# Gate blocks and recurrence values moved to the front of a hybrid decoder layer, as wide blocks with partly seven products

## The chip, the cores and the metric

The kernel runs on one core of one Trainium2 chip. The metric is the device time of one execution in microseconds. TensorE multiplies, VectorE and ScalarE do the elementwise work, POOL (GpSimd) does some of it, SyncE's queue issues the loads of weights. All data is float32; a float32 operand is split into a rounded high part and a remainder ("low"), and a product is made of three passes: high by high, high by low, low by high.

## The reference, cut to what matters

One decoder layer on 256 positions of width 2048:

```
a    = RMSNorm(x)
proj = a @ w_in                        # 17408 columns: q, k, v of attention (3 x 3072),
                                       # q, f, i, g of the recurrence (4 x 1024),
                                       # gate_a, gate_r (2 x 2048)
attn = dilated window attention of 3 head groups, 8 heads, mixed by their denominators
r    = gated linear recurrence over chunks, 8 heads, RMSNorm per head, times silu(g)
y    = sigmoid(gate_a) * (attn @ w_attn_branch) + sigmoid(gate_r) * (r @ w_hgrn_branch)
h    = x + RMSNorm(y @ w_mix_out)
ff   = (silu(gt) * up) @ w_ffn_down,  gt, up = split(RMSNorm(h) @ w_ffn_gate_up)
out  = h + RMSNorm(ff)
```

Every gate is one linear projection of `a`, so gates can be computed at any time before `y`.

## The kernel before

Weights stream once from DRAM. The unit of streaming is 512 KB (a chunk); two chunks share one raw buffer and there are three such buffers. ScalarE rounds a chunk (L242), VectorE takes the remainder (L243), TensorE multiplies. A narrow block ("N", `Block`) is 512 output columns: eight steps of 12 products, two halves of 128 positions, each accumulating in its own PSUM bank. A "W" block is 256 columns computed transposed, four steps. A wide block (`Wide`) is 1024 columns as two groups of 512, one step for each pair of 128-row weight tiles; its raw step is 1 MB. In a plain wide step there are 24 products (2 halves x 2 groups x 2 tiles x 3 passes). In a seven-product step the 2 x 2 block product is done with seven block products instead of eight, 21 in all: VectorE forms sums of the weights (L310, L316, L317), ScalarE rounds them (L315, L318, and L320 for the plain weights still needed), VectorE takes the remainders (L321 `wl`, L322 `dl`), and sums of the activations (`seven_sums`, L374 to L385) stand ready. `gather` collects four of the banks at the last such step, and the block's evacuation adds the rest.

Work is issued in one fixed order. The main loop runs over all steps; at step n it issues the split of step n+2, the load of what is three raw buffers ahead, the products of step n, and then advances generators by one turn each: `evacs` (evacuations of finished blocks), `turns` (transposes of y), and two `lanes` (opening, recurrence and attention on `lanes[0]`, attention and gate sigmoids on `lanes[1]`). Each engine executes its instructions in that order, so the step in which a generator's turn is issued sets where it stands in an engine's queue. A tile's buffer is given to the next tile when all accesses of the old one are done. `flush` issues all remaining turns of a queue at once.

The order of blocks is: output gate g (two N blocks, beside them `opening` with the norms and small tables, L515), f and q of the recurrence (W), its values i (two N blocks, COL_IR), then twice v (three N), q and k (W), then gate_a and gate_r (eight N blocks), then for each of four column blocks j the attention branch and the recurrence branch (8 row tiles, four steps each), the mix projection (`mix`, four N blocks), the first gate and up block (N), ten wide blocks of the feed-forward part, two wide blocks of 22 steps of the down projection. The recurrence starts when the second q block is evacuated; attention for half of the heads starts when that half's last k block is evacuated, two heads in each lane, each head 16 turns. Gates that are evacuated before the heads are done are held as they are (`waiting`) and get their sigmoid behind the heads on `lanes[1]` (`gate_sigmoids`, L934), since Exp and Sigmoid need different ScalarE tables. `evac_g` (L626) multiplies with `gainr`, loaded by `opening` at L518. The mix projection takes y through `yT[0].after(turns)`, which pulls a missing piece (`turned`, L422; `put`, L407) at once.

In the down projection every step first splits its activations: `prep_act` (L1176) puts high and low parts, and for a seven-product step forms the sums, all ahead of the weights' split. At the end `finish` sums, squares, normalises and stores the last columns.

Of the kernel before, what the change touches and what calls it, by code (L numbers as in the profile page):

```python
# [19 lines left out]
P = 128  # L20
# [16 lines left out]
H7 = (0, 1, 2)  # L37
GATE_UP = [(3, 0), (4, 0), (0, 1), (5, 0), (1, 1), (6, 0), (2, 1), (7, 0)]
DOWN = [[(m, m in by7) for m in range(KF // 2)] for by7 in (range(4, 20, 3), range(3, 19, 3))]

N_RAW, N_SPLIT, AHEAD, WARM, BRIDGE = 6, 3, 2, 8, 6
# [20 lines left out]
class Wide:  # L62
# [7 lines left out]
    def __init__(self, w, cols, order, xs, seven, evac, prep=None, pre=None, turn=1):  # L70
# [3 lines left out]
        self.bank, self.open, self.rest = {}, set(), None  # L74
# [3 lines left out]
def tile_hybrid_block(ctx: ExitStack, tc: tile.TileContext, t, out):  # L78
# [8 lines left out]
    auxp = ctx.enter_context(tc.tile_pool(name="auxp", bufs=4, space=PSUM))  # L87
    ctx.enter_context(tc.manual_schedule())
# [19 lines left out]
    def p3(s, dtype, n, bufs, tag=None):  # L108
        return act_pool[0].tile([P, n], dtype, tag=tag or s, bufs=bufs, name=nm(s))
# [48 lines left out]
    ph1 = ExitStack()  # L158
    kp = ph1.enter_context(tc.tile_pool(name="kp", bufs=1, reuse_waits="tile"))
    fp = ph1.enter_context(tc.tile_pool(name="fp", bufs=1, reuse_waits="tile"))  # L160

    act_pool = []

    def fslot(s):
        return fp.tile([P, 1024], F32, tag="f", bufs=15, name=nm(s))

    def ptile(s):
        pool, n = (act_pool[0], 2) if act_pool else (fp, 5)
        return pool.tile([P, 512], F32, tag="p", bufs=n, name=nm(s))
# [13 lines left out]
    blocks, chunks, pairs = [], [], []  # L183
    wides, steps = [], []

    def add(*args, **kw):
        b = Block(*args, **kw)
        blocks.append(b)
        for c in range(b.steps):
            chunks.append([b, c, None, None, None])  # L190
# [15 lines left out]
    def parts(j):  # L206

        return (slice(0, 512), slice(512, 1024)) if j == 0 else (slice(0, 1024),)

    def load(j):  # L210
        if j >= len(chunks):
            load_wide(j - len(chunks))
            return
        b, c = chunks[j][:2]
        if j % 2 == 0:
            pairs.append(stream.tile([P, 2048], F32, tag="raw", bufs=N_RAW // 2, name=nm("raw")))
        raw = pairs[j // 2][:, j % 2 * 1024 : j % 2 * 1024 + 1024]
        rows = b.per * P
        src = b.w[c * rows : (c + 1) * rows, b.col : b.col + b.width]
        src = src.rearrange("(k p) c -> p k c", p=P)  # L220
        dst = raw.rearrange("p (k c) -> p k c", k=b.per)
        n = len(parts(j))
        for i in range(n):
            ks = slice(i * b.per // n, (i + 1) * b.per // n)
            nc.sync.dma_start(dst[:, ks, :], src[:, ks, :])
        chunks[j][2] = raw
# [4 lines left out]
    def split(j, only=None):  # L231
        if j >= len(chunks):
            split_wide(j - len(chunks))
            return
        raw = chunks[j][2]
        if chunks[j][3] is None:
            w = wslot()
            chunks[j][3:] = [w[:, :1024], w[:, 1024:]]
        wh, wl = chunks[j][3:]
        for n, k in enumerate(parts(j)):  # L240
# [4 lines left out]
    def multiply(j, sides=(0, 1)):  # L245
        b, c = chunks[j][:2]
        wh, wl = (w.rearrange("p (k c) -> p k c", k=b.per) for w in chunks[j][3:])
        if b.banks is None:
            b.banks = [acc_bank() for _ in range(2)]
        for s in sides:  # L250
# [23 lines left out]
    def add_wide_block(*args, **kw):  # L274
        b = Wide(*args, **kw)
        wides.append(b)
        for i in range(len(b.order)):
            steps.append([b, i, None, None])

    def load_wide(n):  # L280
        if n % 2 or n // 2 >= len(steps):
            return
        n //= 2
        b, i = steps[n][:2]
        m = b.order[i][0]
        raw = stream.tile([P, 2048], F32, tag="raw", bufs=N_RAW // 2, name=nm("raw"))
        for g, col in enumerate(b.cols):
            src = b.w[2 * m * P : (2 * m + 2) * P, col : col + 512]
            nc.sync.dma_start(
                raw[:, g * 1024 : (g + 1) * 1024].rearrange("p (k c) -> p k c", k=2),  # L290
                src.rearrange("(k p) c -> p k c", p=P),
            )
        steps[n][2] = raw

    def split_wide(n):

        if n >= len(steps):
            return
        b, i, raw = steps[n][:3]
        m, by7 = b.order[i]  # L300
        if b.prep:
            b.prep(m, by7)
        hi, lo = wslot(), p3("wl", F32R, 2048, 3)
        if not by7:
            nc.scalar.activation(hi, raw, AF.Copy)  # L305
            nc.vector.tensor_sub(lo, raw, hi.bitcast(F32))  # L306
            steps[n][3] = hi, lo
# [10 lines left out]
        nc.scalar.activation(hi[:, 1024:], s[:, 1024:], AF.Copy)  # L318
        dhi, dlo = p3("dh", F32R, 1536, 1), p3("dl", F32R, 1536, 1)
        nc.scalar.activation(dhi, d, AF.Copy)  # L320
        nc.vector.tensor_sub(lo, s, hi.bitcast(F32))  # L321
        nc.vector.tensor_sub(dlo, d, dhi.bitcast(F32))  # L322
        steps[n][3] = hi, lo, dhi, dlo

    def multiply_wide(n, sides=(0, 1), groups=(0, 1)):
        b, i = steps[n][:2]
        m, by7 = b.order[i]
        parity = wides.index(b) % 2
# [1097 lines left out]
```

## Time and profile before

| | us |
|---|---|
| median of three runs | 1753.55 (1753.36 to 1753.64) |
| the profiled execution | 1753.68 |
| its span, first to last instruction | 1751.9 |
| TensorE busy | 1730.3 (99%) |
| VectorE busy | 1265.1 (72%) |
| ScalarE busy | 885.0 (51%) |
| POOL busy | 74.1 (4%) |

Matmul ends are modelled and matmuls are pipelined, so TensorE's busy share hides short waits; the time between the starts of products tells more. Instruction rows give start, duration, engine, line, out<-in, shape, and in square brackets the idle time before it with what ended it. Window rows give the length, then the busy time and the number of instructions of PE (TensorE), PEld (its weight loads), DVE (VectorE), ACT (ScalarE) and POOL, then the granted clock, and the DMA share and rate.

### The profile page before, as it was taken

The page shows a single profiled execution, that of the slowest core. Times are in us where ns is not written, and L with a number is a line of the kernel's source. Part 1 is how long each engine was busy: PE and PEld are TensorE (multiplying, and loading weights), DVE is VectorE, ACT ScalarE, POOL GpSimd, SP SyncE. Part 2 cuts the span into 40 slices and gives each one's busy share as a digit, 9 for nine tenths or more (in the row PEclk, how much of TensorE's full clock was granted, in tenths as well). Part 3 has the DMA queues.
Part 4 walks back from the last instruction along what each step waited for, and adds up shares of the span by engine and source line. Part 5 has one row for each costly group of instructions (what it writes and reads, how often), then busy time and mean ns, then how long its engine had stood idle before and what let it go on. Part 6 is the DMA issues. An engine that isn't in the chain of part 4 may idle for free.

```text
span 1751.9 us, 21592 instructions
## 1 busy us (share of the span) xinstructions
PE 1730.3 (99%) x8424; PEld 1449.0 (83%) x8424; DVE 1265.1 (72%) x1372; ACT 885.0 (51%) x1050; POOL 74.1 (4%) x54
## 2 busy tenths in 40 slices
PE   9999999999999999999999999999999999999997
PEld 7888888888888888888888877888888888878775
DVE  5657657877546775544565577888888888888887
ACT  6545445344444444454444465555555555565563
POOL 0002404300000000000000000000000000000000
PEclk9999999999999999999999999999999999999999
DMA  7655444455455554455555745555555555656553
GB/s 265 204 191 193 144 162 151 145 165 182 159 169 169 189 188 161 159 175 193 194 183 189 268 157 203 194 192 193 204 206 204 201 194 192 223 181 218 183 183 117
DMA packets 201223, 325.92 MB, mean 186 GB/s; under 512 B 10096, under 2 KB 76832, under 8 KB 201120
## 3 DMA queue, kind: packets, MB, share of 16 engines
q1 hardware_dynamic: 198848, 319.41, 54.2%
q10 hardware_dynamic: 2272, 5.12, 0.8%
q8 instruction: 66, 1.08, 0.2%
q14 instruction: 37, 0.30, 0.1%
HBM read 322.40 MB, written 2.10 MB: 185 GB/s over the span
## 4 chain that ended last, share of the span: by engine, by line
PE 82%; DVE 12%; ACT 3%; issue 2%; DMA 1%; POOL 0%; SPq 0%; DVEq 0%; ACTq 0%
PE acc L115 65%; PE aux L115 16%; DVE wl L306 3%; DVE wl L321 1%; DVE dl L322 1%; DVE a L411 1%; DVE sum L310 1%; ACT w L318 1%; DVE w L243 1%; DVE sum L317 0%; DVE sum L316 0%; ACT w L242 0%; DVE w L667 0%; ACT so L384 0%; DVE s L379 0%
## 5 line engine op out<-in xcount | busy, mean ns | idle before, releaser
L243 DVE TENSOR_TENSOR w<-raw,w 128x1024 fp32r<-128x1024 f32 (+1 forms) x353 | 444.2, 1260 | 366.4 <-ACT w L242 364.3
L242 ACT ACTIVATE w<-raw 128x1024 fp32r<-128x1024 f32 (+1 forms) x353 | 373.0, 1057 | 483.1 <-PE acc L115 472.1
L115 PE MATMUL acc<-w,xT 128*128 128x512 f32 x1728 | 407.9, 394 | 0.0
L115 PEld LDWEIGHTS acc<-w,xT 128*128 128x128 f32 x1728 | 325.1, 190 | 65.7 <-DVE w L243 0.3
L115 PE MATMUL acc<-xT,w 128*128 128x512 f32 (+1 forms) x2048 | 365.5, 340 | 0.0
L115 PEld LDWEIGHTS acc<-xT,w 128*128 128x128 f32 x2048 | 314.8, 189 | 46.1
L306 DVE TENSOR_TENSOR wl<-raw,w 128x2048 fp32r<-128x2048 f32 x82 | 187.4, 2285 | 19.9 <-ACT w L305 19.9
L305 ACT ACTIVATE w<-raw 128x2048 fp32r<-128x2048 f32 x82 | 156.4, 1908 | 59.0 <-PE aux L115 27.0
L115 PE MATMUL acc<-w,hT 128*128 128x512 f32 x622 | 182.5, 392 | 1.5 <-DVE w L243 1.2
L115 PEld LDWEIGHTS acc<-w,hT 128*128 128x128 f32 x622 | 115.8, 188 | 27.0 <-DVE w L243 2.5
L115 PE MATMUL aux<-w,hT 128*128 128x512 f32 x430 | 135.6, 389 | 0.0
L321 DVE TENSOR_TENSOR wl<-sum,w 128x2048 fp32r<-128x2048 f32 x42 | 96.3, 2292 | 47.3 <-ACT w L318 47.3
L115 PEld LDWEIGHTS aux<-w,hT 128*128 128x128 f32 x430 | 80.7, 188 | 16.8
L315 ACT ACTIVATE w<-sum 128x1024 fp32r<-128x1024 f32 x42 | 44.6, 1063 | 96.3 <-DVE sum L310 92.0
L115 PE MATMUL acc<-w,yT 128*128 128x512 f32 x384 | 88.0, 390 | 0.2 <-DVE w L243 0.2
L115 PEld LDWEIGHTS acc<-w,yT 128*128 128x128 f32 x384 | 71.9, 188 | 15.4 <-DVE w L243 0.6
L115 PE MATMUL acc<-w,a 128*128 128x512 f32 x268 | 83.7, 389 | 0.0
L115 PE MATMUL aux<-w,a 128*128 128x512 f32 x268 | 83.7, 389 | 0.0
L115 PE MATMUL aux<-wl,hT 128*128 128x512 f32 x215 | 83.6, 389 | 0.0
L115 PE MATMUL acc<-wl,hT 128*128 128x512 f32 x215 | 83.6, 389 | 0.0
L322 DVE TENSOR_TENSOR dl<-raw,dh 128x1536 fp32r<-128x1536 f32 x42 | 73.5, 1751 | 0.0
L320 ACT ACTIVATE dh<-raw 128x1536 fp32r<-128x1536 f32 x42 | 61.9, 1473 | 0.0
(263 smaller groups left out, 2016.9 us busy)
## 6 DMA issues: line engine op xcount, KB each, us to landing
raw<-in_w_in SPq DMA_DIRECT2D x271, 512.0 KB, 4.5
raw<-in_w_ffn_gate_up SPq DMA_DIRECT2D x176, 512.0 KB, 4.4
raw<-in_w_ffn_down SPq DMA_DIRECT2D x88, 512.0 KB, 4.9
raw<-in_w_mix_out SPq DMA_DIRECT2D x32, 512.0 KB, 4.9
raw<-in_w_attn_branch SPq DMA_DIRECT2D x16, 512.0 KB, 4.6
raw<-in_w_hgrn_branch SPq DMA_DIRECT2D x16, 512.0 KB, 4.6
hx<-in_x ACTq DMA_DIRECT2D x4, 512.0 KB, 9.9
x<-in_x SPq DMA_DIRECT2D x3, 512.0 KB, 10.4
```

Of the source, the lines that this page charges most:

```text
L115: nc.tensor.matmul(ps, lhsT, rhs, start=start, stop=stop, skip_group_check=True)
L242: nc.scalar.activation(wh[:, k], raw[:, k], AF.Copy)
L243: nc.vector.tensor_sub(wl[:, k], raw[:, k], wh[:, k].bitcast(F32))
L305: nc.scalar.activation(hi, raw, AF.Copy)
L306: nc.vector.tensor_sub(lo, raw, hi.bitcast(F32))
L310: nc.vector.tensor_sub(s[:, :1024].rearrange("p (a c) -> p a c", a=2), raw[:, 512:1536].rearrange("p (a c) -> p a c", a=2), raw[:, None, : ...
L315: nc.scalar.activation(hi[:, :1024], s[:, :1024], AF.Copy)
L318: nc.scalar.activation(hi[:, 1024:], s[:, 1024:], AF.Copy)
L320: nc.scalar.activation(dhi, d, AF.Copy)
L321: nc.vector.tensor_sub(lo, s, hi.bitcast(F32))
L322: nc.vector.tensor_sub(dlo, d, dhi.bitcast(F32))
L411: nc.vector.tensor_sub(x[:, :, 1, :], src, x[:, :, 0, :].bitcast(F32))
```

## The change

The first three gate blocks of 1024 columns (both of gate_a and the first of gate_r) and the recurrence's values i (1024 columns) leave their places and become four wide blocks right behind the two output gate blocks. Each has eight steps, three of them (row pairs 0, 1, 2) by seven products. `pair_sums` forms the activation sums of xT for these pairs in `lanes[1]`, started at steps 6 and 7 of the first output gate block. The gates are evacuated with their sigmoid and stored in a DRAM tile (`kept`) from ScalarE's queue, and read back by `back` on POOL's queue: two when the recurrence branch begins, two in its middle, two at the second attention block. Only the second half of gate_r stays behind the projections (two N blocks). The four recurrence blocks are multiplied first, then the four attention blocks; the flush of the lanes and evacuations stands at the first attention block. The evacuations of the last two recurrence blocks wait until the sigmoids are done. SBUF pools are now "early", "middle" and "late".

Two more edits: `prep_act` becomes a generator whose parts are issued between the instructions of the weights' split, and `down_gain` of the last columns is issued before the normalisation's factor instead of between the stores.

The core of the diff:

```diff
+    def pair_sums(x, which, store, slot):
+        for m in which:
+            f = ptile("f").rearrange("p (k t) -> p k t", k=2)
+            xs = x.slots[m]
+            nc.vector.tensor_add(f, xs[:, :, 0, :].bitcast(F32), xs[:, :, 1, :].bitcast(F32))
+            dst = slot().rearrange("p (z n t) -> p z n t", z=2, n=4)
+            yield
+            seven_sums(f, dst)()
+            store[m] = sums_of(dst)
+            yield
...
     def more_x(c):
         if c + 2 < KD // 2:
             transpose_in(xt, colg, xT, c + 2)
+        else:
+            lanes[1].append(pair_sums(xT, X7[c - 6 :: 2], x7, lambda: rslot("so")))
...
+    def evac_kept_gate(key):
+        def go(b):
+            kept[key] = dram.tile([P, 2, 1024], F32, name=nm("kept"))
+            for s, g in ((0, 0), (0, 1), (1, 0), (1, 1)):
+                e = b.rest[s, g]
+                nc.vector.tensor_add(e, b.bank[s, g], e)
+                nc.scalar.activation(e, e, AF.Sigmoid, scale=r1c[:, s : s + 1])
+                nc.scalar.dma_start(kept[key][:, s, g * 512 : (g + 1) * 512], e)
+            yield
+        return go
+
+    def back(key, j):
+        d = gates[key, j] = nslot("gate")
+        nc.gpsimd.dma_start(d, kept[key, j // 2][:, :, j % 2 * 512 : j % 2 * 512 + 512])
...
     def evac_rec_branch(j):
         def go(banks):
+            part[j] = hslot("part")
+            while j >= 2 and not sigmoids_done[0]:
+                yield
             for i in range(2):
+                nc.vector.tensor_mul(part[j][:, i, :], banks[i], gates["r", j][:, i, :])
                 yield
         return go
...
+    early = [(COL_GA, evac_kept_gate(("a", 0))), (COL_GA + 1024, evac_kept_gate(("a", 1))),
+             (COL_GB, evac_kept_gate(("r", 0))), (COL_IR, evac_i)]
+    for n, (col, ev) in enumerate(early):
+        add_seven(w_in, (col, col + 512), EIGHT, xT, lambda m: x7[m], ev, flip=n % 2 == 1, turn=1,
+                  pre=(lambda: (flush(lanes[0]), flush(lanes[1]))) if n == 0 else None)
...
-    for half in range(2):
-        add("N", w_in, KD, COL_IR + 512 * half, xT, scaled(iN, half, r1c, hslot))
...
-    for j in range(4):
-        add("N", w_in, KD, COL_GA + 512 * j, xT, evac_gate(("a", j), hslot))
-    for j in range(4):
+    for j in (2, 3):
         add("N", w_in, KD, COL_GB + 512 * j, xT, evac_gate(("r", j), fslot))
     for j in range(4):
-        add("N", t["w_attn_branch"][0], 8, 512 * j, attnT, evac_attn_branch(j))
-        add("N", t["w_hgrn_branch"][0], 8, 512 * j, recT, evac_rec_branch(j))
-    blocks[-8].pre = lambda: (flush(lanes[0]), flush(lanes[1]))
+        add("N", t["w_hgrn_branch"][0], 8, 512 * j, lambda k: recT[0](k), evac_rec_branch(j))
+    blocks[-4].pre = lambda: (back("r", 0), back("r", 1))
+    blocks[-2].pre = lambda: (back("a", 0), back("a", 1))
+    for j in range(4):
+        add("N", t["w_attn_branch"][0], 8, 512 * j, lambda k: attnT[0](k), evac_attn_branch(j))
+    blocks[-4].pre = lambda: (flush(lanes[0]), flush(lanes[1]), flush(evacs))
+    blocks[-3].pre = lambda: (back("a", 2), back("a", 3))
...
     def prep_act(m, by7):
         f = act_t[m // 2][:, m % 2 * 2 : m % 2 * 2 + 2, :]
         x = parts_of[m] = Split("a", 2)
-        x.put(0, f)
+        x.high(0, f)
+        yield
+        x.low(0, f)
         if by7:
             dst = rslot("so").rearrange("p (z n t) -> p z n t", z=2, n=4)
-            seven_sums(f, dst)
+            low = seven_sums(f, dst)
             a7[m] = sums_of(dst)
+            yield
+            low()
...
     def split_wide(st):
...
+        prep = b.prep(m, by7) if b.prep else iter(())
+        next(prep, None)
         hi, lo = wslot(), p3("wl", F32R, 2048, 3)
         if not by7:
             nc.scalar.activation(hi, raw, AF.Copy)
+            next(prep, None)
             nc.vector.tensor_sub(lo, raw, hi.bitcast(F32))
...
         nc.scalar.activation(hi[:, 1024:], s[:, 1024:], AF.Copy)
+        next(prep, None)
         dhi, dlo = p3("dh", F32R, 1536, 1), p3("dl", F32R, 1536, 1)
         nc.scalar.activation(dhi, d, AF.Copy)
         nc.vector.tensor_sub(lo, s, hi.bitcast(F32))
+        next(prep, None)
         nc.vector.tensor_sub(dlo, d, dhi.bitcast(F32))
...
     def finish(i, j):
         down_sum(j, i, b)
         down_square(j, i, b)
+        down_gain(j, i, b)
...
         store(2, eng=nc.scalar)
-        down_gain(3, i, b)
         store(3)
```

More of the change, by code (lines that the diff above doesn't have):

```diff
@@ L73, in __init__ @@
         self.last7 = max(i for i, (m, s) in enumerate(order) if s)
-        self.bank, self.open, self.rest = {}, set(), None
+        self.steps = len(order)
+        self.bank, self.open, self.rest, self.flip = {}, set(), None, False
+class Step:
+    def __init__(self, block, i, unit, half):
+        self.block, self.i, self.unit, self.half = block, i, unit, half
+        self.raw = self.parts = None
+        self.last = i == block.steps - 1
 @with_exitstack
@@ L272, in multiply, with split_wide @@
                 mm(b.banks[s][:, :S], l, xh, False, last)
[L274 to L302, printed above, removed]
+    def split_wide(st):
+        b, raw = st.block, st.raw
+        m, by7 = b.order[st.i]
+        prep = b.prep(m, by7) if b.prep else iter(())
+        next(prep, None)
         hi, lo = wslot(), p3("wl", F32R, 2048, 3)
@@ L729, in attention @@
             lo.rearrange("p (j two) -> p two j", two=2), ov,
[L730 removed]
+            attnT[0].f32(4 * half + h).rearrange("p (j two) -> p two j", two=2),
         )
```

296 lines of the change are left out of this document (162 added, 134 removed).

## The prediction

> **What bounds the kernel now.** I read the page first (busy shares, then the chain of work that ended last), then windows cut at the first product of a block, then the timelines of the places that the change touches.
>
> ```profile
> span 1751.9 us, 21592 instructions
> PE 1730.3 (99%) x8424; PEld 1449.0 (83%) x8424; DVE 1265.1 (72%) x1372; ACT 885.0 (51%) x1050; POOL 74.1 (4%) x54
> ...
> PE 82%; DVE 12%; ACT 3%; issue 2%; DMA 1%; POOL 0%; SPq 0%; DVEq 0%; ACTq 0%
> ```
>
> TensorE is busy almost throughout, so a product taken away is time taken away, unless a wait takes its place. The chain's 12% on VectorE say where waits are near. The windows are one narrow block of 512 columns, one wide block of the feed-forward part (1024 columns, three of its eight steps by seven products), the narrow block that enters those wide blocks, and the two blocks of the down projection.
>
> ```profile
> 780.85:802.61 21.76, 21.76 (x97) 18.02 (x96) 9.81 (x8) 9.64 (x10) 0.00 (x0) 1.00 0.55 193
> 1119.31:1161.68 42.37, 42.37 (x193) 35.18 (x191) 36.83 (x31) 22.88 (x20) 0.00 (x0) 1.00 0.58 199
> 1053.00:1076.93 23.93, 22.74 (x97) 17.70 (x96) 17.89 (x31) 14.47 (x16) 0.00 (x0) 1.00 0.52 176
> 1500.83:1620.70 119.87, 118.30 (x520) 96.16 (x518) 104.32 (x110) 70.25 (x69) 0.00 (x0) 1.00 0.62 202
> 1620.70:1741.64 120.94, 117.62 (x511) 95.07 (x509) 105.91 (x122) 66.33 (x73) 0.00 (x0) 1.00 0.50 165
> ```
>
> After each length stand TensorE, its weight loads, VectorE and ScalarE. A narrow block has 96 products of 512 columns in 21.76 us: 0.2267 us each. A wide block of eight steps has 5x24 + 3x21 = 183, or 41.5 us; the feed-forward's 42.37 is that, 8 transposes and hardly a wait. The entering block loses 23.93 - 21.76 = 2.2 us. The down blocks have 510 products each, 115.6 us; they lose 4.3 and 5.3 us, 0.9 of them (as in a feed-forward block) to the first one's transposes, so 8.7 us are waits.
>
> **Fewer products.** Six gate blocks and both blocks of the recurrence's values become four wide blocks. Each of their twelve seven-product steps saves three products: 36 x 0.2267 = **-8.2 us**. VectorE was busy 36.83 of 42.37 us in such a block, with more behind each block than the gates have, so their steady part should not wait (ends -8.2 and -6: half a microsecond per block).
>
> **The front's entry.** Ahead of the first wide block stand the two blocks of the output gate with the opening beside them. Into them come three sets of sums of xT (`pair_sums`), and VectorE works in order there:
>
> ```profile
> 37.83 1.22 DVE L243 TENSOR_TENSOR w<-raw,w 128x1024 fp32r<-128x1024 f32 x1
> ...
> 45.29 0.69 DVE L639 TENSOR_TENSOR g<-sig,gainr 128x512 f32<-128x512 f32 x1 [2.66 <-issue]
> 45.90 2.35 DVE L243 TENSOR_TENSOR w<-raw,w 128x1024 fp32r<-128x1024 f32 x2
> ...
> 49.63 1.42 DVE L542 SCALAR_TENSOR_TENSOR tabs<-cs,rowb 128x256 f32<-128x256 f32 x4
> ...
> 39.49 0.51 SPq L518 DMA_DIRECT2D gainr<-in_hgrn_norm_gain  x1
> ...
> 45.34 5.75 PE L115 MATMUL acc<-w,xT 128*128 128x512 f32 x24
> ```
>
> L639 waits for gainr, which SyncE can issue only behind a weight load, whose buffer the split at 37.83 frees when it ends, at 39.05. A set costs VectorE an addition of 0.7, four sums of 1.0, a wait of 0.7 for ScalarE's rounding and a remainder of 0.7 (rows below, 1547.12 to 1548.11): 3.1 us. Two sets now come before that split; part fits in idle time, and the split ends about 2.2 us later. The load ahead of gainr now has two transfers, for some 1.3 us more. So L639 starts at about 48.7. The split behind it ends at 50.5, but its step started at 45.34 + 2.87 = 48.2 and needs it 0.2 later: 2.0 us lost. Then come the third set, the tables and splits without a pause: the last narrow step loses 2.7. The first seven-product split (7.4 us of VectorE, by L310 to L322 below, and it starts when the split before it ends) loses 1.9, the banks of the second gate block, freed behind it, 2.2, the next seven-product split 1.3. Sum **+10 us**. Lower end 2.2, the feed-forward's own entry with the same three sets; upper end 13, with two spells of half rate (below). I take 10, since the feed-forward's entry has no wait like L639's.
>
> **The turn from recurrence to attention.** Attention's second half starts two steps after the projections end and needs 32 turns, one per step. Before, 64 gate steps covered it. Now there are 32 (two gate blocks, four recurrence blocks of four), so 30 turns are done, and the first attention block begins with a flush: the last head's copies, a table load, two sigmoids, then the products that free the third recurrence block's banks, which the attention block needs.
>
> ```profile
> 759.25 0.40 ACT L727 ACTIVATE attnT<-aux 128x256 fp32r<-128x256 f32 x1 [0.43 <-PE aux L115]
> ...
> 765.81 1.28 ACT L938 ACT_TABLE_LOAD   x1
> 767.10 1.06 ACT L938 ACTIVATE gate<-gate 128x1024 f32<-128x1024 f32 x1
> ...
> 758.97 5.27 PE L115 MATMUL acc<-w,xT 128*128 128x512 f32 x22
> ...
> L948 DVE TENSOR_TENSOR part<-acc,gate x8: 680/683/684, 859.4 to 929.7; 128x512 f32<-128x512 f32 x8
> ```
>
> The step at 758.97 answers to that flush: 759.65 + 1.28 + 1.06 + 0.68 and 0.1 between engines is 762.8, so TensorE stands 3.8 us. After standing it has run at half rate:
>
> ```profile
> 305.10 2.41 PE L115 MATMUL aux<-x 128*128 128x64 f32 x16 [1.41 <-DVE x L766]
> 307.26 4.92 PE L115 MATMUL acc<-xT,w 128*128 128x512 f32 x20
> ```
>
> Twenty products, ten of 512 and ten of 256 columns, should take 3.6 us; 4.92 is 1.3 more. I add 1.2: **+5.0 us**, ends 3.8 and 5.6. The Trainium skill, "TensorE: Matmul & The Clock Gate", Part 1, says that the clock halves after at least one idle window of about 3.4 us, free-running. The 1.41 us before this half rate, with small products behind them, are shorter than that, so the trace does not keep to it. By the page only this flush could halve the clock and the sum stays; by the row the other stalls could too, which is rival 2.
>
> **The mix's inputs.** y is turned by one generator, five steps a block. Blocks used to finish every eight steps, now every four. Counted from the flush, the turns of y0 to y3 start at steps 6, 11, 16 and 21, so the last two pieces are due at mix steps 6 and 7 when their transposes have only just been issued, and are pulled at once. Before, with a step of room:
>
> ```profile
> 944.45 3.89 PE L115 MATMUL acc<-w,yT 128*128 128x512 f32 x16
> ...
> 945.26 0.58 ACT L410 ACTIVATE yT<-aux 128x512 fp32r<-128x512 f32 x1
> ...
> 946.53 0.68 DVE L411 TENSOR_TENSOR yT<-aux,yT 128x512 fp32r<-128x512 f32 x1
> ```
>
> The third product of such a step, due 0.5 after 944.45, would wait until 947.25: 2.3 us, twice: **+4.6 us** (3 to 5.6: the split ahead of them earlier, or the first product waiting for both halves).
>
> **Down projection.** `prep_act` is now spread between the splits' instructions.
>
> ```profile
> 1547.12 0.28 DVE L383 TENSOR_TENSOR s<-act,s 128x128 f32<-128x128 f32 x1
> 1548.11 0.69 DVE L385 TENSOR_TENSOR so<-s,so 128x512 fp32r<-128x512 f32 x1 [0.70 <-ACT so L384]
> 1548.72 1.22 DVE L310 TENSOR_TENSOR sum<-raw 128x1024 f32<-128x1024 f32 x1
> 1549.97 0.69 DVE L316 TENSOR_TENSOR sum<-raw,sum 128x512 f32<-128x512 f32 x1
> 1550.69 0.69 DVE L317 TENSOR_TENSOR sum<-raw,sum 128x512 f32<-128x512 f32 x1
> 1552.52 2.29 DVE L321 TENSOR_TENSOR wl<-sum,w 128x2048 fp32r<-128x2048 f32 x1 [1.13 <-ACT w L318]
> 1554.73 1.75 DVE L322 TENSOR_TENSOR dl<-raw,dh 128x1536 fp32r<-128x1536 f32 x1
> ...
> 1555.86 0.39 PE L115 MATMUL aux<-dh,a 128*128 128x512 f32 x1
> 1556.53 0.50 PE L115 MATMUL aux<-dl,a 128*128 128x512 f32 x1 [0.28 <-DVE dl L322]
> ...
> PE acc L115 <- DVE dl L322: 2.7, 5, 1.6
> PE aux L115 <- DVE dl L322: 1.6, 6, 0.3
> PE acc L115 <- DVE wl L306: 0.7, 1, 0.7
> ```
>
> VectorE goes without a pause but for two waits on ScalarE, 0.70 and 1.13 us, and TensorE then misses `dl` by 0.67 - 0.23 and a restart of 0.1. In the new order other VectorE work fills both waits, so three steps of 5.44 + 5.44 + 4.76 = 15.64 us of products need some 14.4 of VectorE instead of 16.2, and `dl` is ready in time, also behind the first block's evacuation (the 1.6). All 8.7 us of waits should go: **-8.6 us**, ends -9 and -4 (half, if a weight buffer is late next).
>
> **The tail.** The last gain moves from between the stores into VectorE's wait:
>
> ```profile
> 1743.89 0.21 DVE L127 TENSOR_SCALAR v<-fss,base 128x1 f32<-128x1 f32 x1 [0.88 <-ACT junk L1195]
> ...
> 1747.02 0.75 DVE L1200 SCALAR_TENSOR_TENSOR fz<-e,r2c,fpost 128x512 f32<-128x512 f32 x1
> ```
>
> 0.75 fits in 0.88: **-0.7 us** (0 if the stores' transfers bound the end).
>
> **Priced at nothing.** Twelve stores of gates on ScalarE's queue (ScalarE is busy 22.88 of 42.37 us in a wide block); the six reads back on POOL's queue, which holds nothing else there. The nearest transfer of their kind:
>
> ```profile
> hx<-in_x ACTq DMA_DIRECT2D x4, 512.0 KB, 9.9
> ```
>
> A gate is due a block later (10.9 us) and its banks another block later; without that cover each microsecond late is one of TensorE. The recurrence moves 16 steps against the projections, which is a multiple of the four steps of such a block, so its second half meets the same kind of steps: 0, ends -2.5 and +2.5 for stalls such as the 1.41 above. SyncE's loads keep their distance of three buffers.
>
> **Sum.** -8.2 + 10 + 5.0 + 4.6 - 8.6 - 0.7 = +2.1 us. The profiled execution took 1753.68 us (its span 1751.9 and 1.8 around it), 0.13 above the median of the runs; 1753.68 + 2.1 - 0.13 is 1755.6 us.
>
> **Rivals.** 1) *A cheap entry.* The first wide block costs what the feed-forward's costs, 2.2 us: 1747.8 us, faster. For it: the same sets and the same steps. Against it: gainr's wait. It decides once the entry costs less than about 4.4. 2) *Half rate after the other stalls too.* Some four more spells of 1.3 us in the entry and the mix: 1760.8. For it the 1.41 us row, against it the 1.6 us wait for `dl`, which no slow products followed. 3) *The reads back are late.* No row shows a transfer issued by POOL; past 21.8 us after its issue the first one holds the third recurrence block, and 5 us more would give 1760.6. The Trainium skill, "SBUF — State Buffer", section "SBUF: two separate sides", says that GpSimd writes the descriptors of a transfer from POOL's queue itself and cannot while VectorE runs an operation in a two-port mode; no run here shows it. 4) *The down projection keeps its waits*, because something else than VectorE's order makes `dl` late: 1764.2. Against it stand the two pauses and the otherwise unbroken row of VectorE work.
>
> **How the numbers follow.** 0.2% of the time, 3.5 us, is about what can be told from no change. Forecast 0.42, its own range 1751 to 1760 by the ends of its terms; rival 1 0.26; rival 2 0.14; rival 3 0.05; rival 4 0.07; others 0.06. Faster by over 0.2%: most of rival 1 and a little of the forecast and the others, 0.29; within: most of the forecast, 0.31; slower: the rest, 0.40. The range, 1746 to 1763, reaches past rivals 1 and 2 and leaves out rival 4.
>
> **What would show it.** Products fall by 36. TensorE's waits for `dl` in the down blocks vanish and the two blocks take 116 to 117 us each. In the last output-gate block and the first wide block VectorE ends TensorE's waits, some 10 us together, with L639's wait ending near 48.7. A wait of about 3.8 us ends at the first attention block, released by a recurrence `part`; two of about 1 to 1.5 us, followed by shorter ones, stand at mix steps 6 and 7. Wrong would make it above all an entry without the waits, or slow products where I price none.

## The result and the profile after

The changed kernel takes **1764.29 us** (median of 6 runs, 1761.99 to 1768.21) against 1753.6 (median of 6, 1752.66 to 1755.12) before: ratio **1.0062**, 95% interval 1.0049 to 1.0075. It is slower by 10.7 us; the forecast was 1755.6 and its range ended at 1763. The profiled execution took 1761.99 us, its span 1760.2, which is 8.3 above the span before.

The page of the changed kernel (busy times; then the chain, by engine):

```profile
span 1760.2 us, 21616 instructions
...
PE 1725.8 (98%) x8388; PEld 1443.4 (82%) x8388; DVE 1334.8 (76%) x1434; ACT 903.8 (51%) x1051; POOL 77.8 (4%) x60
...
PE 93%; DVE 4%; ACT 2%; issue 1%; DMA 0%; SPq 0%; DVEq 0%; ACTq 0%
```

The 36 products are gone (8424 to 8388), and VectorE's share of the chain fell from 12% to 4%, because the down projection no longer waits for it (2% in the run below that changes the down projection alone). The kernel is slower all the same: shares of a chain do not say where a stage got longer. The windows do; in order: the second output-gate block, the first wide block, a later wide block, eight W blocks beside the second recurrence, the first mix block, the two down blocks.

```profile
32.83:59.68 26.85, 24.31 (x106) 18.76 (x105) 20.68 (x41) 14.21 (x17) 0.00 (x0) 1.00 0.48 165
59.68:107.30 47.62, 43.61 (x184) 33.97 (x183) 40.56 (x40) 25.35 (x22) 0.00 (x0) 1.00 0.64 226
107.30:149.70 42.40, 42.40 (x184) 34.35 (x183) 35.52 (x29) 23.14 (x20) 0.00 (x0) 1.00 0.65 224
455.95:574.33 118.38, 111.62 (x682) 98.93 (x681) 100.78 (x112) 51.61 (x87) 33.77 (x18) 0.97 0.43 143
948.56:976.95 28.39, 24.72 (x114) 19.48 (x112) 14.79 (x16) 10.42 (x12) 0.00 (x0) 1.00 0.51 165
1518.47:1634.97 116.50, 116.50 (x520) 96.55 (x518) 103.90 (x110) 70.95 (x69) 0.00 (x0) 1.00 0.63 208
1634.97:1750.73 115.76, 115.76 (x511) 95.53 (x509) 105.93 (x125) 67.23 (x74) 0.00 (x0) 1.00 0.52 173
```

| part | forecast, us | the two profiled executions, us | how measured |
|---|---|---|---|
| fewer products | -8.2 | -4.5 | four wide blocks at 42.40, each for two narrow ones of 21.76 |
| entry of the front | +10 | +8.9 | 26.85 for 23.19, and 47.62 for 42.40 |
| turn to attention's branch | +5.0 | +5.3 | a wait of 3.58, then 1.7 of half rate |
| mix's inputs | +4.6 | +4.1 | four waits, 3.67, and four restarts of 0.1 |
| recurrence | 0 | **+4.5** | V blocks and first half's Q and K blocks, 249.4 for 244.9 (before: with the values' blocks, less 43.5 for their own products) |
| down projection | -8.6 | -8.55 | 232.26 for 240.81 |
| tail | -0.7 | -0.7 | from the last product to the end |
| the first blocks | not named | -0.8 | they start 0.5 earlier and run 0.3 shorter |
| sum | +2.1 | +8.2 | the spans differ by 8.3 |

To these come 2.3 us by which the median run of the changed kernel lies above its profiled one. Each run's mean granted clock goes with its time: 0.996 at 1761.99, 0.994 at 1763.37, 1764.01 and 1764.57, 0.993 at 1765.21, 0.991 at 1768.21.

What the text calls half rate is this clock: in the profile of the changed kernel it is 0.50 from 472.17 to 479.00 and from 902.25 to 905.66, in the profile before from 306.47 to 309.88 and from 333.77 to 337.19, always in stretches of 3.41 us or twice that. The second stretch of the kernel before follows no wait: 32 small products in a row (of 64 columns and of 1 column) stand ahead of it. The forecast, made from this trace, saw only the first.

**Steps that came as forecast.** The wait at the turn to the attention branch, and the first pair of mix waits (TensorE's timeline of the changed kernel; in brackets the idle time before and what ended it):

```profile
901.46 4.84 PE L129 MATMUL acc<-w,attnT 128*128 128x512 f32 x13 [3.58 <-DVE part L1036]
```

```profile
967.59 0.74 PE L129 MATMUL acc<-w,yT 128*128 128x512 f32 x2 [1.19 <-ACT yT L457]
968.97 2.56 PE L129 MATMUL acc<-w,yT 128*128 128x512 f32 x10 [0.64 <-DVE yT L461]
```

In the down projection no wait of TensorE is left, and VectorE's row through a seven-product split has no pause:

```profile
1565.30 2.29 DVE L352 TENSOR_TENSOR wl<-sum,w 128x2048 fp32r<-128x2048 f32 x1
1567.50 0.68 DVE L417 TENSOR_TENSOR so<-s,so 128x512 fp32r<-128x512 f32 x1
1568.10 1.75 DVE L354 TENSOR_TENSOR dl<-raw,dh 128x1536 fp32r<-128x1536 f32 x1
```

The stores and the reads back, listed by the median time from issue to landing, are hidden as priced: 5.8 us against a cover of 21.8.

```profile
kept<-e ACTq DMA_DIRECT2D x12, 256.0 KB, 4.4
gate<-kept POOLq DMA_DIRECT2D x6, 512.0 KB, 5.8
```

In the entry gainr is issued at 41.27 instead of 39.49, and VectorE, in order, stands 2.06 us; then the three sets, the tables and the splits pile up (VectorE's row, then TensorE's):

```profile
46.84 0.69 DVE L725 TENSOR_TENSOR g<-sig,gainr 128x512 f32<-128x512 f32 x1 [2.06 <-issue]
```

```profile
48.72 2.81 PE L129 MATMUL acc<-w,xT 128*128 128x512 f32 x11 [0.56 <-DVE w L295]
...
55.80 0.49 PE L129 MATMUL acc<-w,xT 128*128 128x512 f32 x1 [1.13 <-ACT w L294]
57.06 2.79 PE L129 MATMUL acc<-w,xT 128*128 128x512 f32 x11 [0.77 <-DVE w L295]
```

**The step that did not.** In the second recurrence TensorE stands 5.07 us at 467.42, then runs at half rate. VectorE and POOL there, and the product that waited:

```profile
459.13 0.75 DVE L238 TENSOR_TENSOR sum<-acc,sum 128x256 f32<-128x256 f32 x2
462.07 2.62 DVE L753 TENSOR_TENSOR w<-sum,tabs 64x512 f32<-64x512 f32 x2
464.73 2.81 DVE L295 TENSOR_TENSOR w<-raw,w 128x1024 fp32r<-128x1024 f32 x1
467.45 0.68 DVE L759 TENSOR_TENSOR sum<-sum,tabs 128x512 f32<-128x512 f32 x1
468.17 1.87 DVE L760 TENSOR_TENSOR qk<-sum,w 128x512 f32<-128x512 f32 x1
469.96 2.38 DVE L851 TENSOR_TENSOR x<-x,kk 128x512 f32<-128x512 f32 x1
```

```profile
458.24 2.73 POOL L845 TENSOR_TENSOR x<-b 128x1024 f32<-128x1024 f32 x1 [53.85 <-DVE b L837]
464.12 2.34 POOL L845 TENSOR_TENSOR x<-b 128x1024 f32<-128x1024 f32 x1
467.86 1.63 POOL L852 TENSOR_TENSOR x<-x,q 128x512 f32<-128x512 f32 x1 [1.41 <-ACT x L849]
469.45 2.34 POOL L845 TENSOR_TENSOR x<-b 128x1024 f32<-128x1024 f32 x1
```

```profile
472.48 3.65 PE L129 MATMUL aux<-x 128*128 128x64 f32 x16 [5.07 <-DVE x L851]
```

A split's subtraction (L295) takes 1.22 elsewhere; here 2.81. It starts at 464.73, inside POOL's 464.12 to 466.46, and ends at 467.54, about 1.1 behind POOL's end. L851 (0.69 elsewhere) starts at 469.96, inside 469.45 to 471.79, and ends at 472.34. VectorE does not run slowly; it seems to stand until POOL is done. L238, one input of which is a PSUM bank (`acc`), takes its usual 0.75 in the middle of POOL's 458.24 to 460.97. The kernel before shows the same, in the rows ahead of the 1.41 us wait that the forecast quoted: two operations that take 1.38 together took 4.16.

```profile
295.81 4.16 DVE L667 TENSOR_TENSOR w<-sum,tabs 64x512 f32<-64x512 f32 x2
```

```profile
295.73 1.28 POOL L767 TENSOR_TENSOR x<-x,q 128x512 f32<-128x512 f32 x1 [1.95 <-ACT x L764]
296.96 2.47 POOL L760 TENSOR_TENSOR x<-b 128x1024 f32<-128x1024 f32 x1
```

### The profile page after: what moved, and what is told of

Same layout as the page of the kernel before. It is cut to its first block, busy times and chain, and to the rows that moved or that the text cites. A ratio compares the mean times of both kernels' runs of the same rounds, so it can differ in the third digit from the quotient of the medians.

```text
span 1760.2 us, 21616 instructions
## 1 busy us (share of the span) xinstructions
PE 1725.8 (98%) x8388; PEld 1443.4 (82%) x8388; DVE 1334.8 (76%) x1434; ACT 903.8 (51%) x1051; POOL 77.8 (4%) x60
## 4 chain that ended last, share of the span: by engine, by line
PE 93%; DVE 4%; ACT 2%; issue 1%; DMA 0%; SPq 0%; DVEq 0%; ACTq 0%
PE acc L129 65%; PE aux L129 26%; DVE w L295 1%; DVE w L753 1%; ACT w L294 1%; PE aux L799 0%; PE aux L493 0%; ACT w L334 0%; DMA x<-in_x 0%; PE acc L1188 0%; DVE fz L1315 0%; DVE wl L336 0%; PE aux L1188 0%; DVE x L851 0%; ACT junk L1269 0%
## 5 line engine op out<-in xcount | busy, mean ns | idle before, releaser
L295 DVE TENSOR_TENSOR w<-raw,w 128x1024 fp32r<-128x1024 f32 (+1 forms) x289 | 366.0, 1268 | 284.2 <-ACT w L294 282.1
L294 ACT ACTIVATE w<-raw 128x1024 fp32r<-128x1024 f32 (+1 forms) x289 | 305.0, 1056 | 393.7 <-PE acc L129 380.3
L129 PE MATMUL acc<-w,xT 128*128 128x512 f32 x1132 | 286.4, 396 | 2.4 <-DVE w L295 1.3
L336 DVE TENSOR_TENSOR wl<-raw,w 128x2048 fp32r<-128x2048 f32 x102 | 233.3, 2287 | 41.3 <-ACT w L334 40.3
L129 PEld LDWEIGHTS acc<-w,xT 128*128 128x128 f32 x1132 | 213.7, 191 | 47.1 <-DVE w L295 2.1
L334 ACT ACTIVATE w<-raw 128x2048 fp32r<-128x2048 f32 x102 | 194.7, 1909 | 96.0 <-PE aux L129 41.1
L352 DVE TENSOR_TENSOR wl<-sum,w 128x2048 fp32r<-128x2048 f32 x54 | 123.7, 2291 | 50.8 <-ACT w L348 48.5
L345 ACT ACTIVATE w<-sum 128x1024 fp32r<-128x1024 f32 x54 | 57.4, 1063 | 151.5 <-DVE sum L340 150.1
L354 DVE TENSOR_TENSOR dl<-raw,dh 128x1536 fp32r<-128x1536 f32 x54 | 94.6, 1752 | 0.0
L351 ACT ACTIVATE dh<-raw 128x1536 fp32r<-128x1536 f32 x54 | 79.6, 1474 | 0.0
```

Source lines behind the costliest of these rows:

```text
L129: nc.tensor.matmul(ps, lhsT, rhs, start=start, stop=stop, skip_group_check=True)
L294: nc.scalar.activation(wh[:, k], raw[:, k], AF.Copy)
L295: nc.vector.tensor_sub(wl[:, k], raw[:, k], wh[:, k].bitcast(F32))
L345: nc.scalar.activation(hi[:, :1024], s[:, :1024], AF.Copy)
```

## The experiments

Theory: the second recurrence's levels now meet rope's work on VectorE, and POOL holds VectorE up; the rest is as forecast, but for the wide products' pace. Rivals: buffers or transfers that the change brought hold the recurrence up; VectorE has too much work there; the waits' half rate is the whole excess. Each experiment edits the changed kernel unless it says otherwise.

**The values back as narrow blocks.**

```
-early = [..., (COL_GB, evac_kept_gate(("r", 0))), (COL_IR, evac_i)]
+early = [..., (COL_GB, evac_kept_gate(("r", 0)))]
+for half in range(2):                    # behind the query blocks
+    add("N", w_in, KD, COL_IR + 512 * half, xT, scaled(iN, half, r1c, hslot))
```

> The changed kernel with the recurrence's values (IR) back as two narrow blocks behind the query blocks; three gate blocks stay in front. The recurrence then starts 16 steps earlier against the projections, as it did before. Theory (the recurrence's levels meet rope's VectorE work because of the 16 steps): the 5.07 us wait in the last step of block Q010 and the products at half rate behind it are gone, the second recurrence costs 4 to 5 us less, and the two narrow blocks cost 1.1 us more than the wide one (43.5 against 42.4): about 1761 us. Rival (the wait comes from something else that the change brought, such as buffers of the new pool): a wait of about 5 us stays somewhere in the second recurrence, 1765 us.

1759.37 us (4 runs), ratio 1.0044 (1.0029 to 1.0059): 4.9 us less by the medians. The 5.07 us wait is gone. The eight blocks of the second recurrence that answer to 455.95 to 574.33 take 111.48 us instead of 118.38 (113.18 before); more recurrence stands beside the narrow values again, so the stretch from the values' blocks (those alone) and V to the last of these costs 2.0 us less in all, 3.1 without the 1.1 of the wide block. That is less than the 4 to 5 expected; the clock is halved for 10.2 us of this stretch, in the changed kernel for 6.8, which hides a part of the gain. The 16 steps are the condition; the rival with the new buffers falls.

**POOL's work in the second recurrence given to VectorE.**

```
 def recurrence(half):
+    eng = nc.vector if half else nc.gpsimd
-    nc.gpsimd.tensor_sub(...)   nc.gpsimd.tensor_mul(...)   # in the levels
+    eng.tensor_sub(...)         eng.tensor_mul(...)
```

> The changed kernel with the operations of the second recurrence's levels that POOL runs (subtractions and products, 1.3 to 2.7 us each) moved to VectorE. Theory (the 5.07 us wait at 467 comes from VectorE's operations running at half speed beside POOL's): VectorE's rope and level operations take their usual 0.68 to 1.4 us there, the wait falls below 2 us, and the second recurrence's blocks lose 3 to 5 us less. Rival (VectorE simply has more work than time in those steps): the wait stays at 5 or grows, since VectorE gets the work of POOL as well; other steps of the second recurrence get slower.

1756.24 us (10 runs), ratio 1.0016 (1.0006 to 1.0025): 8.0 us less, with more work on VectorE; the stretch of eight blocks alone takes 6.8 less, more than the 3 to 5 expected. Its rows in the same place (VectorE, then the whole stretch of eight blocks as a window):

```profile
464.45 1.38 DVE L753 TENSOR_TENSOR w<-sum,tabs 64x512 f32<-64x512 f32 x2
465.86 1.23 DVE L295 TENSOR_TENSOR w<-raw,w 128x1024 fp32r<-128x1024 f32 x1
467.00 0.69 DVE L759 TENSOR_TENSOR sum<-sum,tabs 128x512 f32<-128x512 f32 x1
467.72 0.69 DVE L760 TENSOR_TENSOR qk<-sum,w 128x512 f32<-128x512 f32 x1
468.33 0.69 DVE L852 TENSOR_TENSOR x<-x,kk 128x512 f32<-128x512 f32 x1
468.94 0.69 DVE L853 TENSOR_TENSOR x<-x,q 128x512 f32<-128x512 f32 x1
469.54 1.22 DVE L846 TENSOR_TENSOR x<-b 128x1024 f32<-128x1024 f32 x1
```

```profile
458.23:569.83 111.60, 110.46 (x682) 97.44 (x681) 96.11 (x130) 51.38 (x87) 0.00 (x0) 0.98 0.46 151
```

Every operation is back at its usual time, and TensorE no longer waits there; one wait of 1.0 us is left later in the stretch, at 484.9. VectorE does POOL's 1.63 in 0.69 and its 2.34 in 1.22, and with 18 operations more it is busy 96.11 us instead of 100.78, since being held up counts as busy. So VectorE had time; POOL took it away. The Trainium skill, "SBUF — State Buffer", section "SBUF: two separate sides", says that VectorE with two inputs in SBUF and a GpSimd (POOL) operation that reads SBUF lock each other out for a whole instruction, the later one standing still. The ends above, 467.54 and 472.34, agree with that.

**Idle products behind the flush.**

```
-pre = lambda: (flush(lanes[0]), flush(lanes[1]), flush(evacs))
+pre = lambda: (flush(lanes[0]), flush(lanes[1]), flush(evacs), keep_warm(14))
```

> The changed kernel with 14 idle products (about 3 us) issued on TensorE at the end of the flush, ahead of the first attention-branch block. Theory (half rate follows from TensorE standing still): the wait for the third recurrence block's banks stays where it ends, about 897.9 us, but the first step of that block takes 2.7 to 2.9 us instead of 4.45, the total falls by 1.6 us to about 1762.7. Rival (the first products are slow by themselves or for another cause): the step stays at 4.4, no gain.

The wait ends where it did, and the step behind it falls from 4.45 to 2.86. But now the second pair of mix waits, after which the changed kernel's first profile shows no slow products, is followed by seven, 1.49 us. 1763.18 us (4 runs, 1762.03 to 1767.17): no gain that can be told. Half rate is a matter of when, not of which wait.

**Two turns a step.**

```
-if turns and type(turns[0]) is not list: advance(turns)
+for _ in range(2):
+    if turns and type(turns[0]) is not list: advance(turns)
```

> The changed kernel with the queue of y's turns advanced twice a step instead of once. Theory (the last two pieces of y are turned too late for mix steps 6 and 7): the four waits in the first mix block (1.2 + 0.6, twice) and its products at half rate go, the block falls from 28.4 to 23 to 24 us, the total by about 4.4 to 1760. Rival (the mix waits for the branch products' evacuation, not for the turns): 3 us or more of waits stay in that block.

1759.02 us (5 runs), ratio 1.0037 (1.0023 to 1.0051): 5.3 less. The first mix block as a window:

```profile
951.60:974.44 22.84, 22.84 (x107) 18.84 (x106) 14.28 (x15) 11.23 (x12) 0.00 (x0) 1.00 0.56 184
```

TensorE is busy throughout; with what moved into the blocks around it, the profile gives -4.4, as forecast.

**gainr early.**

```
+nc.scalar.dma_start(gainr, ...)     # at the start of opening()
 yield from sumsq(ss, xt)
-nc.sync.dma_start(gainr, ...)
```

> The changed kernel with gainr's load issued on ScalarE's queue at the start of the opening instead of on SyncE behind the weight loads. Theory (VectorE standing for gainr makes everything behind it late): the output gate's product no longer waits, and the second output-gate block and the first wide block together lose 5 to 6 us instead of 8.9, total about 1761. Rival (VectorE has more work there than time, with or without gainr): less than 1 us gained.

The second output-gate block takes 24.83 instead of 26.85, the first wide block 47.60 as ever: 2.0 us instead of 3 to 4; 1762.26 us (4 runs). The sums and splits in the wide block are a jam of their own.

**Pace by the operands' place.**

```
 enter("early")
+pool["now"].tile([P, 112], F32, tag="pad", bufs=1, name="pad")   # 448 bytes; 16, 176, 240 below
```

> The changed kernel with 448 bytes left free at the bottom of the front's pool, so that the low weight parts (wl) and the differences (dh, dl) start 192 bytes past a multiple of 1024, as every other operand of the products does, instead of 768. Theory (the front's wide blocks take 42.40 us instead of 41.5 because of where these operands lie): their steps fall from 5.57 to 5.44 and from 4.83 to 4.76, three and a half blocks gain 3.2 us, about 1761. Rival (the pace is a state left behind by the waits in the entry, whatever the addresses): 42.4 us again, 1764.

The later wide blocks fall to 41.48 us, and every product starts 226 or 227 ns after the one before, where the changed kernel wanders between 224 and 241. There all products of the block are slow, also those of `w` with `xT`, which touch no low part: one such product starts 229 to 241 ns after the other. The total does not follow: 1764.15 us (4 runs, granted clock 0.990 to 0.994). Its profile holds 12.4 us of half rate against 4.3 in the changed kernel's. Three further paddings, one execution each:

> The changed kernel with 64 instead of 448 bytes left free at the bottom of the front's pool: the low parts then lie 832 bytes past a multiple of 1024, which is 64 past a multiple of 128 (as all other operands) but not 192 past a multiple of 256. If the distance in 128 bytes is what sets the pace, the front's wide blocks take 41.5 us; if it is in 256 or more, 42.4.

> The changed kernel with the front's low parts 448 bytes past a multiple of 1024 (704 bytes left free): 192 past a multiple of 256, but not of 512, where all other operands lie 192 past a multiple of 512. If the distance in 256 bytes sets the pace of the front's wide blocks, they take 41.5 us; if that in 512 or more does, 42.3.

> The same with 704 bytes past a multiple of 1024 (960 bytes left free): 192 past a multiple of 512. If 512 sets the pace, 41.5 us a block; if 1024, 42.3.

The window of a later wide block in the runs with 448, 64, 704 and 960 bytes left free (one fence each):

```profile
107.25:148.73 41.48, 41.48 (x184) 34.35 (x183) 35.52 (x29) 23.16 (x20) 0.00 (x0) 1.00 0.65 228
```

```profile
108.11:150.39 42.28, 42.28 (x185) 34.37 (x183) 35.52 (x29) 23.13 (x20) 0.00 (x0) 1.00 0.64 225
```

```profile
106.97:148.45 41.48, 41.48 (x184) 34.35 (x183) 35.52 (x29) 23.14 (x20) 0.00 (x0) 1.00 0.66 228
```

```profile
106.75:148.23 41.48, 41.48 (x185) 34.35 (x184) 35.52 (x29) 23.14 (x20) 0.00 (x0) 1.00 0.66 229
```

Low parts 192, 448 or 704 bytes past a multiple of 1024 run at full pace; 768 (as changed) and 832 do not. The three good ones are 192 past a multiple of 256, as all other operands of these products are. Whether 192 itself matters or being alike does was not tried. Nor was the place of the low parts by itself: the padding moves all tiles of the front's pool, VectorE's sums of the weights among them. The idea that a disturbance sets the pace was tried by itself:

```
 w = st.parts
+if i == 0 and pool["name"] == "early":
+    mm(bank((0, 0))[:, :64], act_of(0, 0)[0], w[0][:, :64], True, False)
```

> The changed kernel with one product of 64 columns more at the start of each of the four wide blocks in the front (its result is overwritten). Theory (pace by operands' places): the blocks stay at 42.4 us and the extra product's 0.1. Rival (pace by a state of TensorE that a disturbance sets): in one or more of the three later blocks the products return to 226.7 ns, 41.6 us a block.

The later wide blocks' steps stay at 5.6 and 4.83: that idea falls. (Its 1769.67 us is one execution.)

**The down projection alone**, on the kernel before:

```
-if b.prep: b.prep(m, by7)
+prep = b.prep(m, by7) if b.prep else iter(()); next(prep, None)    # and two more next(prep, None)
 ... down_square(j, i, b)
+down_gain(j, i, b)                                                 # instead of between the stores
```

> The kernel before with one part of the change alone: the preparation of the down projection spread between the splits' instructions, and the last gain moved ahead of the stores. By the prediction's two terms (-8.6 and -0.7) it takes 9.3 us less than the kernel before: ratio 0.9947. Rival (the waits went for another reason, such as loads that stand elsewhere after the front was rebuilt): a gain of less than 3 us.

**1743.76 us** (4 runs), ratio 0.9944 (0.9928 to 0.9961): 10.0 us less by the medians; its down blocks take 116.50 and 115.76, as in the changed kernel. Of the 10.2 us between the profiles 8.55 lie there, 1.1 in the tail and 0.8 in the first blocks, which the edit does not touch. This part is worth what the forecast said, wherever the front stands.

**The causes together.** The five edits (POOL, turns, gainr, padding of 448, idle products):

> The changed kernel with five edits together: no POOL work in the second recurrence's levels, two turns of y a step, gainr's load early, the front's low parts 192 bytes past a multiple of 1024, idle products behind the flush. If these causes are separate, their gains against the changed kernel add up: 8.0 + 5.3 + 2.0 (by the medians of the single runs), 3.6 (by the blocks' times) and 1.6, some 20 us, so about 1744. Rival (the gains overlap, or half rate behind the remaining waits gives them back): 1748 to 1752.

1744.46 us (4 runs), ratio 0.9948 (0.9934 to 0.9963): 19.8 us less than the changed kernel. The gains add up as expected and show no overlap. They are not all measured one by one, though: by the medians of the single runs padding and idle products gave only 0.1 and 1.1, and the sum would be 16.6. Half rate is the likely difference: the granted clock is 0.996 to 0.999 here and 0.991 to 0.996 in the changed kernel, and at 0.996 the two take 1745.57 and 1746.53 against 1761.99, about 16 us apart.

**POOL's work in the order before**, on the kernel of the down projection alone:

> The kernel before with the change's part in the down projection, and with the second recurrence's level operations moved from POOL to VectorE. Theory (POOL's operations slow VectorE's there too, and the 1.41 us wait at 303.7 with its half rate comes from it): that wait goes, 1.5 to 3 us less than the 1743.8 of the run without this edit. Rival (in the old order VectorE has work enough): no gain or up to 2 us lost.

**1738.94 us** (4 runs), ratio 0.9920 (0.9905 to 0.9934): 4.8 less, more than expected. The 1.41 us wait is gone, and no half rate is left behind the first microseconds of the profile. A part of the 4.8 is that clock: it is 0.998 in three of the runs, and in the fourth 0.996, as in all runs without the edit; that fourth run took 1741.95, only some 2 us less than they did.

**Two wide blocks instead of four**, first behind narrow values, then behind the forget blocks (the order in short, not the lines of the edit):

```
+# GR0 GR1 [IR0 IR1 | F00..F11] with one set of sums every four steps, then
-early = [GA01, GA23, GB01, IR]
+early = [GA01, GA23]                    # all four recurrence gates late and narrow
```

> As the run with the five edits, but without the idle products, and with another order: the recurrence's values as two narrow blocks right behind the output gate, the sums of xT one set every four steps beside them, then only the two pairs of attention-gate blocks as wide blocks, and all four recurrence gates late as narrow blocks. Theory (the entry is lost because VectorE has the opening and the sums at once; the flush is lost because only 32 steps cover attention's 32 turns): the entry's 6.9 us and the flush's 5.3 us nearly vanish, two wide blocks still save 4.1 us, about 1737. Rival (VectorE's late work moves to the next block, or the reads back of two gates are late): 1743 or more.

> Two wide blocks of attention gates in the front, behind the forget blocks, with the sums of xT spread beside those; the recurrence's values back behind the queries, so that the recurrence stands against rope as in the kernel before; each recurrence gate waited for by itself; and as before no POOL work in the second recurrence's levels, two turns a step, gainr's load early, the low parts shifted. If the recurrence's place and the sigmoids are what the run with two wide blocks still loses (2.8 and 2.1 us against the run that only took POOL's work from the old order), it takes 1735 to 1736 us; if VectorE is late beside the forget blocks, 1739 or more.

1739.98 us, ratio 0.9920 (0.9903 to 0.9936), and 1739.82, ratio 0.9930 (0.9914 to 0.9947), 4 runs each. The first enters the wide blocks at no cost at all: the output-gate block takes 23.19 and the wide one 41.48.

```profile
33.34:56.53 23.19, 23.19 (x106) 18.99 (x105) 16.24 (x32) 13.29 (x17) 0.00 (x0) 1.00 0.58 194
100.05:141.53 41.48, 41.48 (x185) 34.36 (x183) 35.58 (x27) 21.60 (x18) 0.00 (x0) 1.00 0.65 229
```

The second puts the recurrence back in its place and loses 2.7 us in its first wide block instead, a wait of 2.1 for `dl`. The first misses its expectation by 3 us; the second lands where it was expected if VectorE is late, at 1739 or more. Both are level with the run that saved no product in the front. That products saved there bring anything was therefore not shown.

**The changed kernel profiled again.**

> The changed kernel as it is, profiled a second time, for the spells of products at half rate behind its waits. If such a spell is bound to the wait, it follows the same waits as in the first profile (those that end at 472.5 and 901.5 alone); if it depends on where a wait falls in a window that runs by itself, other waits have one too, and the span differs by the sum of the spells.

Span 1761.3. Half rate, added over products that took twice their time, comes to 6.8 us against 4.3, in other places: behind the waits at 57 (1.3 us), and at 391.6 (1.5), where no wait stands. TensorE there in the first profile, then in the second; 48 products each (one record is missing in the first):

```profile
387.48 1.89 PE L129 MATMUL aux<-x 128*128 128x64 f32 x16
389.21 1.90 PE L129 MATMUL aux<-ones,x 128*128 128x1 f32 x16
390.97 11.32 PE L129 MATMUL acc<-w,xT 128*128 128x512 f32 x47
```

```profile
387.39 1.89 PE L129 MATMUL aux<-x 128*128 128x64 f32 x16
389.12 1.90 PE L129 MATMUL aux<-ones,x 128*128 128x1 f32 x16
390.88 12.98 PE L129 MATMUL acc<-w,xT 128*128 128x512 f32 x48
```

What comes before is 32 small products in a row. The span grew by 1.1, not by 2.5: the spell at 57 cost nothing, since VectorE sets the end there (entry 74.45 us in the second profile, 74.47 in the first).

## Why the prediction was wrong

- **The failed step** is the one priced at nothing: "a multiple of the four steps of such a block, so its second half meets the same kind of steps: 0, ends -2.5 and +2.5". It measured +4.5, outside those ends. The count of 16 was right; the steps are not alike. A block's rope work runs in the steps of the next one. Before, the second recurrence's first levels fell on the first block of 256 query columns, ahead of which stands a V block, without rope; now they fall on the fifth, with rope in full ahead of it. And the price of an encounter was read from the wait it left (1.41), not from the rows that caused it: the 4.16 above stood in the trace of before.
- **Mis-sized: fewer products**, -8.2, measured -4.5. "Their steady part should not wait" holds; it does not wait. Each product takes 232 ns instead of the 226.7 taken from other blocks, and it goes back to 226.7 when the front's pool is moved so that the low parts start 192 instead of 768 bytes past a multiple of 1024.
- **Half rate (rival 2)** is real, but not bound to stalls as it assumed. By the clock that goes with the runs' times it is also why the median lies 2.3 us above the profiled run. By the Trainium skill, "TensorE: Matmul & The Clock Gate", Part 1, the window runs freely and the count of slow products changes from run to run: the two profiles agree. That a whole idle window is needed they do not bear out: the spell at 391.6 follows 32 small products without a wait, and so does the one at 333.8 of the kernel before.
- **Right within 1.2 us each**: the entry (8.9 for 10; L639's wait, L725 in the changed kernel, ended at 46.84, not 48.7: the split ahead ended 1.3 later instead of 2.2, and the second transfer cost SyncE 0.5 instead of the 1.3 allowed; gainr is worth 2.0 of the 8.9), the flush (5.3 for 5.0), the mix (4.1 for 4.6), the down projection (8.55 for 8.6), the tail. Rivals 1, 3 and 4 fall: the entry is not cheap, the reads back landed in 5.8 us, the down projection kept no wait. That the result lies at rival 4's 1764.2 is chance.
- In sum: 1755.6, + 4.5 recurrence, + 3.7 pace, + 2.3 half rate in the median run, - 1.8 in the other terms, the first blocks and rounding, is 1764.3.

## What to carry to other kernels

When work is moved against other work, ask at both places which engines run what beside it, and read the durations of the operations there, not the wait that happens to be left: an operation that takes twice or three times its usual time can name a lock before it becomes a stall. Take a product's pace only for operands that lie as they will lie. And try a change's parts alone: here the reordering in the down projection was worth 10 us by the medians and, with POOL's work taken away, 14.5 (0.9920), more than the whole rebuilt front could show.

## What the hardware showed unexpectedly

- Beside POOL's operations VectorE's operations with two inputs in SBUF look stopped rather than slowed: 2.81 for 1.23 us, 2.38 for 0.69, each ending 0.1 less than its usual duration behind POOL's. The same work took VectorE about half of POOL's time (0.69 for 1.63, 1.22 for 2.34).
- fp32 products of 128x512, one after another, start every 226.7 ns in blocks with all operands 192 bytes past a multiple of 256, and every 231 to 232 with the low parts 0 or 64 past. The V blocks, which read every second position of xT, start them every 233 to 235 on average in both kernels, with operands 192 past; why was not tried.
- TensorE's half rate (granted clock 0.50, in stretches of 3.41 us) came after waits of 1.0 to 5 us or after 32 small products without a wait, in some executions and not in others, 1.2 to 1.7 us a stretch as a rule. Between profiles the sum went from none to 12.4 us.
